# mLSTM heads in chunks of 256 tokens with three carried states, and two column sums folded into one set of matrix products

## The chip, the cores and the metric

One core of one Trainium2 chip. TensorE (PE) multiplies matrices, VectorE (DVE), ScalarE (ACT) and GpSimd (POOL) do elementwise work, and SyncE (SP) issues the DMAs. The built program sets the order of the instructions on each engine, and semaphores tell an instruction when what it needs is there. The metric is device microseconds of the whole program, a median over runs.

## The reference

One decoder layer over 1024 tokens of width 1024, in float32: an RMS norm, a projection into four mLSTM heads of width 128 and eight forgetting-attention heads of width 64, an output projection, cross-attention into 256 memory tokens, an MLP with squared ReLU, and a final norm. The change concerns the mLSTM heads. Each has a causal convolution with SiLU on q and k, input and forget gates, and a recurrence that the reference runs in chunks of 64 tokens:

```
scores = einsum('bhtd,bhsd->bhts', qc, kc) * exp(dmat - m_t[..., None])
num = einsum('bhts,bhsd->bhtd', scores, vc) + inter * einsum('bhed,bhtd->bhte', C, qc)
den = scores.sum(-1) + inter * einsum('bhd,bhtd->bht', n, qc)
h = num / maximum(abs(den), exp(-m_t))
C_new = decay * C + einsum('bhs,bhse,bhsd->bhed', wa, vc, kc)
n_new = decay * n + einsum('bhs,bhsd->bhd', wa, kc)
```

C is a 128 x 128 state, n a vector, m a running maximum. A kernel may choose another chunk length: inside a chunk the scores are computed directly, across chunks the state carries. The head's output is then normalised by its mean square and gated.

## The kernel before, in words

Every product with full precision is done as three products of rounded halves (`mm3`, lines 192 to 194): each operand is split into a high part, rounded by ACT (line 138), and a low remainder, subtracted by DVE (line 139).

The mLSTM part runs over four heads. For one head, `ml_project` (lines 666 to 687) does: `conv_silu` of k (projection in 48 products of 512 columns, two evictions by DVE at line 522, four taps at lines 525 and 527, tanh on ACT at line 529, line 530, and the split at lines 141 and 142), `fx_project(0)`, the state of the first 512 tokens in `carried` (four transposes at line 545, eight products at line 551), `conv_silu` of q, `fx_project(1)`, the state's effect on the second 512 tokens in `carry`, and the output gate's projection. `ml_head` then computes scores and values in two halves of 512 tokens; within a half the four key blocks reach 512, 384, 256 and 256 query columns. The sums over the 128 partitions of the squares and of the denominators are products with a column of ones (`sum_cols`, line 232), four for each of the two in each half.

The closing of a head (from line 628 on) is a generator which the next head's `ml_project` advances between its steps: the 8 x 128 factors are transposed on PE (line 257), copied (line 258), stored to `facd`, read back as a broadcast to all partitions for the first half (line 261) and then for the second (line 637), and DVE scales the head's output with them (lines 640 and 641). The broadcasts share one buffer, `r_a`.

The order of all this on each engine is not written by hand here. A scheduler in the tile framework places instructions by program order and by its own estimate of when each can start, and assigns buffers from pools: PSUM has one bank tagged mm, one m2, two tp, three sc and one ov, and `mm()` hands out mm, tp, m2, tp in turn. A tile that takes a bank waits for the last reader of the tile before it there. Small SBUF buffers have tags too (`r_c`, `r_b`, `r_f` two each, `r_a` one).

Of the kernel before, what the change touches and what calls it, by code (L numbers as in the profile page):

```python
# [44 lines left out]
def hybrid_layer(ctx: ExitStack, tc: tile.TileContext, a: dict, out: bass.AP):  # L45
# [50 lines left out]
    def ov_():  # L96
        return ps_tile("ov")
# [22 lines left out]
    ones = const("ones", [P, 1])  # L120
    g.memset(ones, 1.0)
# [167 lines left out]
    def mem_prepare():  # L289
# [16 lines left out]
        rsqrt_sums(acc, rcol_m, 2, 2)  # L306
# [152 lines left out]
    left = dram.tile([MLH, TH], F32, name="left")  # L459
# [4 lines left out]
    def gate_rows():  # L464
# [21 lines left out]
        w = run[0:MLH, 0:TH]  # L486
        s.activation(w, rel[0:MLH, 0:TH], AF.Exp, bias=neg[0:MLH, TH - 1 : TH])
# [46 lines left out]
    def carried(hd, y):  # L534

        cols = col("m", 8, 1)
        m0, m1, n_ = (cols[:, i : i + 1] for i in range(3))
        load(m0, rows[hd : hd + 1, TH - 1 : TH].broadcast_to([P, 1]))

        kw = w2("b")  # L540
        load(kw, left[hd : hd + 1].broadcast_to([P, TH]))
        v.scalar_tensor_tensor(out=kw, in0=y[:, :TH], scalar=0.5 * float(P) ** -0.5, in1=kw, op0=ALU.mult, op1=ALU.mult, accum_out=n_)
        kt = mm() if hd else ov_()
        for j in range(4):
            nc.tensor.transpose(kt[:, j * P : (j + 1) * P], kw[:, j * P : (j + 1) * P], ident)
        kh, kl = w2("d", dt=F32R), w2("e", dt=F32R)
        split(kh, kl, kt)
        ps = mm()
        for j in range(4):
            for t in (kl, kh):  # L550
                nc.tensor.matmul(ps[:, 0:256], t[:, j * P : (j + 1) * P], mv_of(hd, j), start=j == 0 and t is kl, stop=j == 3 and t is kh)
        c32 = w2("c", P)
        s.activation(c32, ps[:, P : 2 * P], AF.Copy)
        v.tensor_tensor(out=c32, in0=ps[:, 0:P], in1=c32, op=ALU.add)
        c2 = w2("p", 2 * P, F32R)
        hi, lo = c2[:, 0:P], c2[:, P:]

        v.tensor_scalar(out=n_, in0=n_, scalar1=0.5, scalar2=None, op0=ALU.mult)
        v.tensor_scalar(out=m1, in0=m0, scalar1=-1.0, scalar2=None, op0=ALU.mult)
        split(hi, lo, c32)  # L560
        return m1, (hi, lo), n_

    def carry(hd, q, y, m1, c, n_):

        e = w2("c")
        load(e, rows[hd : hd + 1, TH:].broadcast_to([P, TH]))
        s.activation(e, e, AF.Exp, bias=m1)
        ps = mm()
        mm3(ps, c, both(q, lambda t: t[:, TH:]), True, True)
# [1187 lines left out]
```

## Time and profile before

| | |
|---|---|
| median of 3 runs | 1512.55 us (1512.06 to 1512.98) |
| profiled execution, span | 1510.9 us |
| TensorE busy | 1498.5 us, 99% |
| VectorE busy | 1097.5 us, 73% |
| ScalarE busy | 717.5 us, 47% |
| GpSimd busy | 450.6 us, 30% |

The profiled execution's own time is its span, 1510.9 us from the first to the last instruction; the median of the runs is 1.65 us above it. The four heads lie between about 60 and 370 us. In the rows of the timeline the columns are start, duration, engine, line, operation, output <- inputs, shape, count, and in brackets the idle time ahead with what ended it. In the rows by stretch each engine's busy time stands with its number of instructions, then the granted TensorE clock, the DMA share and GB/s.

### The profile page before, as it was taken

The numbers are of one execution on the slowest core, as the hardware profiler recorded it, in microseconds if no ns is written. First come the engines' busy times: TensorE is split into PE (matmuls) and PEld (weight loads), VectorE is DVE, ScalarE is ACT, GpSimd is POOL, SyncE is SP. The second block draws the span as 40 slices with busy tenths as digits, with TensorE's granted clock in tenths as the row PEclk, the third lists the DMA queues.
The fourth block names the chain that finished last, engine by engine and source line by source line (L and its number), as shares of the span: only waits on it lengthen the run. The fifth ranks groups of instructions, "written<-read, shape, count | busy, mean of one in ns | idle before, by whom it ended". The sixth has DMA issues, their size and how long they took to land.

```text
span 1510.9 us, 21868 instructions
## 1 busy us (share of the span) xinstructions
PE 1498.5 (99%) x7708; PEld 1259.5 (83%) x7708; DVE 1097.5 (73%) x1743; ACT 717.5 (47%) x1347; POOL 450.6 (30%) x529
## 2 busy tenths in 40 slices
PE   9999999999999999999999999999999999999997
PEld 8988888889999888888888888888888888888887
DVE  7676676665799875844457988888887788777765
ACT  7343343334788773534444556565656332222134
POOL 0003030413466551001110033344433644343312
PEclk9999999999999999999999999999999999999999
DMA  5332333436889768533334446867766865555623
GB/s 209 117 114 91 115 100 127 129 130 169 279 253 270 218 199 291 198 123 119 119 119 133 154 136 237 281 244 265 272 243 235 352 258 221 223 223 223 251 84 112
DMA packets 114258, 288.33 MB, mean 191 GB/s; under 512 B 12882, under 2 KB 23436, under 8 KB 108516
## 3 DMA queue, kind: packets, MB, share of 16 engines
q1 hardware_dynamic: 113860, 286.83, 56.0%
q8 instruction: 60, 0.98, 0.3%
q14 instruction: 50, 0.41, 0.1%
q10 hardware_dynamic: 288, 0.11, 0.0%
HBM read 194.36 MB, written 92.53 MB: 190 GB/s over the span
## 4 chain that ended last, share of the span: by engine, by line
PE 98%; issue 0%; DVE 0%; DMA 0%; POOL 0%; ACT 0%; POOLq 0%; ACTq 0%; DVEq 0%
PE tp L194 9%; PE tp L193 9%; PE tp L192 9%; PE sc L192 7%; PE sc L194 7%; PE sc L193 7%; PE m L192 6%; PE m L194 6%; PE m L193 6%; PE mm L192 6%; PE mm L193 6%; PE mm L194 6%; PE ov L813 2%; PE ov L192 2%; PE ov L193 2%; PE ov L194 2%
## 5 line engine op out<-in xcount | busy, mean ns | idle before, releaser
L194 PE MATMUL tp<-act,wh 128*128 128x512 f32 (+1 forms) x456 | 178.5, 392 | 0.0
L192 PE MATMUL tp<-act,wl 128*128 128x512 f32 (+1 forms) x456 | 178.5, 392 | 0.0
L193 PE MATMUL tp<-act,wh 128*128 128x512 f32 (+1 forms) x456 | 178.5, 391 | 0.0
L138 ACT ACTIVATE wh<-wr 128x1024 fp32r<-128x1024 f32 (+3 forms) x96 | 92.7, 966 | 95.9 <-PE tp L194 36.6
L139 DVE TENSOR_TENSOR wl<-wr,wh 128x1024 fp32r<-128x1024 f32 (+3 forms) x96 | 113.9, 1187 | 14.5 <-ACT wh L138 14.4
L193 PE MATMUL mm<-act,wh 128*128 128x512 f32 (+1 forms) x320 | 122.6, 383 | 0.0
L192 PE MATMUL mm<-act,wl 128*128 128x512 f32 (+1 forms) x320 | 122.6, 383 | 0.0
L194 PE MATMUL mm<-act,wh 128*128 128x512 f32 (+1 forms) x320 | 122.3, 382 | 0.0
L192 PE MATMUL m<-act,wl 128*128 128x512 f32 (+1 forms) x312 | 119.5, 383 | 0.0
L193 PE MATMUL m<-act,wh 128*128 128x512 f32 (+1 forms) x312 | 118.9, 381 | 0.0
L194 PE MATMUL m<-act,wh 128*128 128x512 f32 (+1 forms) x312 | 118.8, 381 | 0.0
L192 PE MATMUL sc<-act,wl 128*128 128x512 f32 (+1 forms) x268 | 103.8, 387 | 0.0
L193 PE MATMUL sc<-act,wh 128*128 128x512 f32 (+1 forms) x268 | 103.7, 387 | 0.0
L194 PE MATMUL sc<-act,wh 128*128 128x512 f32 (+1 forms) x268 | 103.6, 387 | 0.0
L194 PEld LDWEIGHTS tp<-act,wh 128*128 128x128 f32 x456 | 85.7, 188 | 19.5
L193 PEld LDWEIGHTS tp<-act,wh 128*128 128x128 f32 x456 | 85.8, 188 | 19.0
L192 PEld LDWEIGHTS tp<-act,wl 128*128 128x128 f32 x456 | 85.7, 188 | 19.0
L1491 POOL TENSOR_TENSOR z<-wr 128x256 f32<-128x256 f32 x56 | 50.4, 921 | 147.6 <-DMA wr<-w_ff2q 140.8
L138 ACT ACTIVATE w<-wr 128x768 fp32r<-128x768 f32 (+2 forms) x31 | 25.5, 825 | 133.7 <-PE tp L194 69.2
L138 ACT ACTIVATE wh<-z 128x1024 fp32r<-128x1024 f32 (+2 forms) x55 | 52.5, 956 | 65.0 <-POOL z L1491 28.8
L139 DVE TENSOR_TENSOR wl<-z,wh 128x1024 fp32r<-128x1024 f32 (+2 forms) x55 | 65.9, 1198 | 10.1 <-ACT wh L138 10.1
L194 PEld LDWEIGHTS mm<-act,wh 128*128 128x128 f32 x320 | 60.2, 188 | 12.5
(673 smaller groups left out, 4207.9 us busy)
## 6 DMA issues: line engine op xcount, KB each, us to landing
act<-right SPq DMA_DIRECT2D x35, 1024.0 KB
right<-r_d SPq DMA_DIRECT2D x70, 256.0 KB
right<-w SPq DMA_DIRECT2D x56, 256.0 KB
wr<-w_ff2q SPq DMA_DIRECT2D x28, 512.0 KB
act<-fqk SPq DMA_DIRECT2D x48, 256.0 KB
wr<-w_in SPq DMA_DIRECT2D x20, 512.0 KB
wr<-w_ff SPq DMA_DIRECT2D x20, 512.0 KB
fqk<-r_p SPq DMA_DIRECT2D x32, 256.0 KB
```

Of the source, the lines that this page charges most:

```text
L138: s.activation(hi, src, AF.Copy)
L139: return v.tensor_tensor(out=lo, in0=src, in1=hi.bitcast(F32), op=ALU.subtract)
L192: nc.tensor.matmul(ps, w[1], x[0], start=first, stop=False, skip_group_check=more)
L193: nc.tensor.matmul(ps, w[0], x[1], start=False, stop=False, skip_group_check=more)
L194: nc.tensor.matmul(ps, w[0], x[0], start=False, stop=last, skip_group_check=more)
L813: nc.tensor.matmul(self.ov[:, c0:], self.fv[:, self.j], t[:, c0:], start=self.j == 0 and t is self.p[1], stop=self.last and t is self.p[0])
L1491: g.tensor_tensor(out=o, in0=x, in1=y, op=op)
```

## The change

Chunks become 256 tokens long, so three states are carried instead of one (after 256, 512 and 768 tokens). `carried` weighs k against three chunk ends, in place in k's own buffer, takes six transposes and twelve products, and combines the three states on DVE with decay factors that ACT exponentiates. `carry` applies them to three chunks of q. In `ml_head` each half consists of two chunks with two key blocks of 256 columns each. The squares and the denominators are each folded from 128 to 64 partitions by DVE, side by side into one tile, and summed by four products with a two-column pattern of ones. The memory's norm folds its sums too. `carry` now stands ahead of `fx_project(1)`.

```diff
+    units_ = const("ones", [P, 3])
+    ones, pair_ones = units_[:, 0:1], units_[:, 1:3]
...
-        rsqrt_sums(acc, rcol_m, 2, 2)
+        v.tensor_tensor(out=acc[:, :NM], in0=acc[:, :NM], in1=acc[:, NM:], op=ALU.add)
+        rsqrt_sums(acc, rcol_m, 2)
...
+    QC = 256
+    left = dram.tile([MLH, 3 * QC], F32, name="left")
...
     def carried(hd, y):
...
-        kt = mm() if hd else ov_()
-        for j in range(4):
-            nc.tensor.transpose(kt[:, j * P : (j + 1) * P], kw[:, j * P : (j + 1) * P], ident)
...
+        cols, more = col("m", 8, 1), col("mx", 8)
+        m0, m1, n_, d = cols[:, 0:3], cols[:, 3:6], more[:, 0:3], more[:, 3:5]
+        load(m0, rows[hd : hd + 1, QC - 1 : 3 * QC : QC].broadcast_to([P, 3]))
+        v.tensor_scalar(out=m1, in0=m0, scalar1=-1.0, scalar2=None, op0=ALU.mult)
+
+        for c in range(2):
+            s.activation(d[:, c : c + 1], m0[:, c + 1 : c + 2], AF.Exp, bias=m1[:, c : c + 1])
...
+        for c in range(3):
+            at = slice(c * QC, c * QC + QC)
+            v.scalar_tensor_tensor(out=y[:, at], in0=y[:, at], scalar=0.5 * float(P) ** -0.5, in1=lw[c // 2][:, c % 2 * QC : c % 2 * QC + QC], op0=ALU.mult, op1=ALU.mult, accum_out=n_[:, c : c + 1])
+        c32 = w2("c", 3 * P).rearrange("p (c d) -> p c d", c=3)
+        for at, n in ((0, 2), (2, 1)):
+            kt = mm() if hd or at else ov_()
+            kt = kt[:, : n * QC]
+            for j in range(2 * n):
+                i = at * QC + j * P
+                nc.tensor.transpose(kt[:, j * P : (j + 1) * P], y[:, i : i + P], ident)
+            kh, kl = w2("d", n * QC, F32R), w2("e", n * QC, F32R)
+            split(kh, kl, kt)
+            ps = mm()[:, : n * QC].rearrange("p (c e d) -> p c e d", c=n, e=2)
...
     def carry(hd, q, y, m1, c, n_):
...
+        for i in range(3):
+            hf, x = divmod(i + 1, 2)
+            x = slice(x * QC, x * QC + QC)
+            z = slice(0, QC) if i == 0 else x
+            s.activation(e[hf][:, z], e[hf][:, z], AF.Exp, bias=m1[:, i : i + 1])
+            mm3(ps[hf][:, z], both(c, lambda t: t[:, i]), both(q, lambda t: t[:, (i + 1) * QC : (i + 2) * QC]), True, True)
...
     def ml_head(hd, q, k, og, nums, accs_):
...
+                for j, z in ends:
+                    mm3(sp[:, z], both(k, lambda t: t[:, j * P : (j + 1) * P]), both(q, lambda t: t[:, hf * TH + c * QC :][:, :QC]), True, True)
...
-            ps = sc()
-            sum_cols(ps[:, 0:4], acc, 4)
-            sum_cols(ps[:, 4:8], sq, 4)
...
+            folded = w2("c")
+            for t, x in ((folded[0:64], sq), (folded[64:128], acc)):
+                v.tensor_tensor(out=t, in0=x[0:64], in1=x[64:128], op=ALU.add)
+            for t in range(4):
+                nc.tensor.matmul(ps[:, t], folded[:, t * P : (t + 1) * P], pair_ones, start=True, stop=True)
...
+        sums = carry(hd, q, yq, *state)
         fx_project(1, hd)
-        sums = carry(hd, q, yq, *state)
```

Lines of the changed kernel move: `mm3` is at 195 to 197, the split at 141 and 142 (144 and 145 with a scale), the conv's eviction at 528, its taps at 531 and 533, tanh at 535 and line 536, the weighing of k at 554, transposes at 561, state products at 569, the carry's loads at 585, the folded sums at 644, the closing's transpose at 260, its copy at 261, its DMAs at 262, 264 and 663, its scaling at 666 and 667.

The order moves in three places. First TensorE at the state of head 1. Before (m_219 is the first half of conv q, mm_1588 the transposed k, tp_1597 the state):

```order
L192 MATMUL m_219_1629<-act_102,wl_1624 128x512
L545 MATMUL mm_1588<-ident,r_b_1585 128x128
L193 MATMUL ov_1335<-r_e_1393,act_106 128x256
L194 MATMUL ov_1335<-r_d_1392,act_106 128x256
L545 MATMUL mm_1588<-ident,r_b_1585 128x128 x3
L193 MATMUL m_219_1629<-act_103,wh_1623 128x512
...
L194 MATMUL m_219_1629<-act_102,wh_1623 128x512
L551 MATMUL tp_1597<-act_106,r_e_1594 128x256
L551 MATMUL tp_1597<-act_106,r_d_1593 128x256
```

In the change (m_197 is the end of fx_project(0), tp_1612 and tp_1632 the transposed k, mm_1621 the states, tp_1670 conv q):

```order
L644 MATMUL sc_1419<-ones,r_c_1420 128x2 x4
L196 MATMUL m_197_1557<-act_107,wh_1521 128x512
L197 MATMUL m_197_1557<-act_106,wh_1521 128x512
L561 MATMUL tp_1612<-ident,z_188_1504 128x128 x4
L561 MATMUL tp_1632<-ident,z_188_1504 128x128 x2
L569 MATMUL mm_1621<-act_108,r_e_1618 128x256
L569 MATMUL mm_1621<-act_108,r_d_1617 128x256
...
L195 MATMUL tp_1670<-act_104,wl_1665 128x512
```

Between the transposes and the first product of the state 17 products of conv q stood before; now none does.

Second, TensorE from conv q to the carry of the same head in the change (mm_1696 is the second half of conv q, mm_1796 the second half of fx_project(1), tp_1739 and m_232_1740 the carry, tp_1764 the first half of fx_project(1); 24 products each for the halves):

```order
L197 MATMUL mm_1696<-act_106,wh_1664 128x512
L195 MATMUL mm_1796<-act_106,wl_1761 128x512
L196 MATMUL mm_1796<-act_107,wh_1760 128x512
...
L197 MATMUL mm_1796<-act_106,wh_1760 128x512
L195 MATMUL tp_1739<-act_1443,r_p_1652 128x256
L195 MATMUL m_232_1740<-act_1443,r_p_1652 128x256
L195 MATMUL tp_1764<-act_104,wl_1761 128x512
```

Before, both halves of fx_project(1) and 22 products of the output gate stood between conv q and the carry; now 24 products do, and they take the bank that conv q has just written.

Third, DVE at the same place. Before:

```order
L522 TENSOR_TENSOR z_218_1627<-tp_1655,row 128x512
L525 TENSOR_SCALAR z_221_1681<-z_218_1627,vec 128x1024
L139 TENSOR_TENSOR wl_2018<-wr_2015,wh_2017 128x1024
L527 SCALAR_TENSOR_TENSOR z_221_1681<-z_218_1627,vec,z_221_1681 128x1024 x2
L653 SCALAR_TENSOR_TENSOR r_p_1721<-mm_1696,row 128x512
L527 SCALAR_TENSOR_TENSOR z_221_1681<-z_218_1627,vec,z_221_1681 128x1024
L640 SCALAR_TENSOR_TENSOR r_f_1319<-r_f_1319,vec,r_a_1498 128x512
L641 SCALAR_TENSOR_TENSOR r_f_1319<-w_131_1188,r_f_1319 128x512
L530 SCALAR_TENSOR_TENSOR z_221_1681<-z_218_1627,z_221_1681 128x1024
```

In the change:

```order
L528 TENSOR_TENSOR z_221_1668<-tp_1670,row 128x512
L666 SCALAR_TENSOR_TENSOR r_f_1140<-r_f_1140,vec,r_a_1513 128x512
L667 SCALAR_TENSOR_TENSOR r_f_1140<-w_142_1233,r_f_1140 128x512
L545 TENSOR_SCALAR c_m_2196<-c_m_2196 128x3
L145 SCALAR_TENSOR_TENSOR r_f_1140<-r_f_1140,r_y_1591 128x512
L666 SCALAR_TENSOR_TENSOR r_f_1141<-r_f_1141,vec,r_a_1596 128x512
L528 TENSOR_TENSOR z_221_1668<-mm_1696,row 128x512
L667 SCALAR_TENSOR_TENSOR r_f_1141<-w_142_1233,r_f_1141 128x512
L142 TENSOR_TENSOR wl_2045<-wr_2042,wh_2044 128x1024
L531 TENSOR_SCALAR z_224_1722<-z_221_1668,vec 128x1024
L145 SCALAR_TENSOR_TENSOR r_f_1141<-r_f_1141,r_y_1657 128x512
L533 SCALAR_TENSOR_TENSOR z_224_1722<-z_221_1668,vec,z_224_1722 128x1024 x3
```

Both scalings of the previous head's closing (L666, with the broadcasts r_a) now stand ahead of the eviction of conv q's second half; before, they stood behind it.

120 lines of the change are left out of this document (58 added, 62 removed).

## The prediction

> **What bounds the kernel now.** I read the page first, then the busy time by stretches.
>
> ```profile
> span 1510.9 us, 21868 instructions
> PE 1498.5 (99%) x7708; PEld 1259.5 (83%) x7708; DVE 1097.5 (73%) x1743; ACT 717.5 (47%) x1347; POOL 450.6 (30%) x529
> ...
> PE 98%; issue 0%; DVE 0%; DMA 0%; POOL 0%; ACT 0%; POOLq 0%; ACTq 0%; DVEq 0%
> ...
> 171.00:241.00 70.00, 70.00 (x340) 58.33 (x339) 47.57 (x75) 25.65 (x43) 14.16 (x18) 1.00 0.34 108
> ```
>
> TensorE is never free, the chain of waits lies on it for 98%, and in the stretch of one mLSTM head (171 to 241 us, the last row) it works 70 of 70 us at full clock while VectorE (DVE) works 47.6. So the time is the sum of the slots that instructions take on TensorE, start to start, plus any wait that a new order puts on it. The timeline gives the slots:
>
> ```profile
> 200.00 0.39 PE L193 MATMUL m<-act,wh 128*128 128x512 f32 x1
> 200.24 0.39 PE L194 MATMUL m<-act,wh 128*128 128x512 f32 x1
> ...
> 201.41 0.34 PE L192 MATMUL sc<-act 128*128 128x384 f32 x1
> 201.59 0.34 PE L193 MATMUL sc<-act 128*128 128x384 f32 x1
> ...
> 203.65 0.28 PE L193 MATMUL ov<-r_e,act 128*128 128x256 f32 x1
> 203.77 0.28 PE L194 MATMUL ov<-r_d,act 128*128 128x256 f32 x1
> ...
> 209.85 0.95 PE L232 MATMUL sc<-ones,r_c 128*128 128x1 f32 x8
> 210.66 0.37 PE L192 MATMUL sc<-act 128*128 128x256 f32 x1
> ...
> 222.41 0.60 PE L545 MATMUL tp<-ident,r_b 128*128 128x128 f32 x4
> 222.76 0.48 PE L192 MATMUL tp<-act,wl 128*128 128x512 f32 x1
> ```
>
> 512 columns take 0.235 us, 384 take 0.177, 256 take 0.12, a column sum 0.10 (eight in 0.81), a transpose 0.09 (four in 0.35). The 0.28 to 0.39 of the rows is latency, and overlaps.
>
> **What TensorE saves.** Scores and values, per half: three products each of 512, 384, 256 and 256 columns, twice: 6 x (0.235 + 0.177 + 0.12 + 0.12) = 3.9 us; now 24 of 256, 2.9. Eight halves: -8.2. Column sums fall from 64 to 32: -3.2. The memory norm's, from 4 to 2: -0.2. The states cost 4 more products of 256 columns and 2 more transposes per head, 4 x (0.48 + 0.18) = +2.6, and the carry 9 x 0.12 against 3 x 0.235, 4 x 0.375 = +1.5. Sum -7.5 us. The folds, the extra exponentials and the chunked splits are on DVE, ACT and POOL, which have 22 us and more of slack in the 70; they cost nothing so long as TensorE does not stand behind them. That is what the new order changes.
>
> **What the order adds: the head's closing.** In the change the product of the second half of conv q writes bank mm, and so does the next block, the 24 products of fx1. There is one such bank, so they wait for the eviction L528, and on DVE L528 now stands behind the second L666, which waits for a broadcast of the head's factors. How long that takes shows in head 0's closing now:
>
> ```profile
> 170.43 0.27 PE L257 MATMUL sc<-ident,c_fac 128*8 128x128 f32 x1
> ...
> 170.73 0.27 ACT L258 ACTIVATE r_a<-sc 8x128 f32<-8x128 f32 x1 [2.77 <-PE sc L257]
> ...
> 171.03 0.28 SPq L259 DMA_DIRECT2D facd<-r_a  x1
> 173.34 0.32 SPq L261 DMA_DIRECT2D r_a<-facd  x1
> 177.35 0.32 SPq L637 DMA_DIRECT2D r_a<-facd  x1
> ...
> 176.57 0.75 DVE L640 SCALAR_TENSOR_TENSOR r_f<-r_f,vec,r_a 128x512 f32<-128x512 f32 x1 [2.08 <-DMA r_a<-facd]
> 180.64 0.75 DVE L640 SCALAR_TENSOR_TENSOR r_f<-r_f,vec,r_a 128x512 f32<-128x512 f32 x1 [0.85 <-DMA r_a<-facd]
> ```
>
> Store 2.3 us, load 3.2, and, since there is one buffer r_a, a second load of 3.3 after the first is used: the second scaling begins 10.2 us after the transpose of the factors and ends at 10.95. L528 (0.69, below) ends at 11.65. After the same transpose TensorE has 5 + 24 products, 0.25 + 29 x 0.235 = 7.05 us. **Wait C: 4.6 us.** If the three DMAs went a quarter faster, 2.4 us would be left of it; if the small load of c_m, which on SP stands ahead of the second factor load and itself follows an exponential, came late by its own 2.7 us (row below), 7.3. The carry's own second load now stands on SP between the store and the load of the factors; it waits for the state's split, 0.4 us after the transpose, and the factor load waits 2.3 us for the store anyway, so it holds nothing up.
>
> **The carry.** It now stands directly behind those 24 products and begins with q's rounded half. What is between the eviction of conv q and that half, in the trace of now:
>
> ```profile
> 166.90 0.69 DVE L522 TENSOR_TENSOR z<-tp,row 128x512 f32<-128x512 f32 x1 [1.41 <-PE tp L194]
> 167.62 0.81 DVE L525 TENSOR_SCALAR z<-z,vec 128x1024 f32<-128x1024 f32 x1
> 168.35 1.22 DVE L139 TENSOR_TENSOR wl<-wr,wh 128x1024 fp32r<-128x1024 f32 x1
> 169.49 2.60 DVE L527 SCALAR_TENSOR_TENSOR z<-z,vec,z 128x1024 f32<-128x1024 f32 x2
> ...
> 177.97 1.22 DVE L530 SCALAR_TENSOR_TENSOR z<-z,z 128x1024 f32<-128x1024 f32 x1
> ...
> 174.58 1.06 ACT L529 ACTIVATE z<-z 128x1024 f32<-128x1024 f32 x1 [3.58 <-DVE z L527]
> 179.22 1.06 ACT L141 ACTIVATE act<-z 128x1024 fp32r<-128x1024 f32 x1 [0.51 <-DVE z L530]
> ...
> 183.13 0.39 PE L192 MATMUL m<-act,r_p 128*128 128x512 f32 x1
> ```
>
> Now q is ready at 180.28, 13.4 us after the eviction began, and its carry is issued at 183.13: 70 products stand between, so nobody waits. In the new order the DVE rows after L528 (shown above) are L667 0.69, a weights split 1.22, L531 0.81, the closing's L145 0.68, three L533 3.9, then tanh 1.06, L536 1.22, ACT's rounding 1.06: 10.6 us, less about 0.08 where one row starts before the one ahead ends: 10.4. TensorE has 24 x 0.235 = 5.6. **Wait D: 4.8 us**; 3.0 without the weights split and L145, 5.5 with some delay at each hand-over. The rest of the carry needs q's remainder, two DVE pieces later, with 20 products ahead of it: covered.
>
> **The states.** The transposes L561 come directly after fx0's last products, and the state products L569 directly after the transposes, since conv q needs the two tp banks that the transposes hold. Nearest rows for the pieces:
>
> ```profile
> 88.39 0.60 ACT L138 ACTIVATE r_d<-ov 128x512 fp32r<-128x512 f32 x1 [1.49 <-PE ov L545]
> ...
> 89.35 0.67 DVE L139 TENSOR_TENSOR r_e<-ov,r_d 128x512 fp32r<-128x512 f32 x1
> 111.02 0.15 DVE L559 TENSOR_SCALAR c_m<-c_m 128x1 f32<-128x1 f32 x1 [1.28 <-DMA c_m<-rows]
> ...
> 108.28 0.39 SPq L538 DMA_DIRECT2D c_m<-rows  x1
> ...
> L823 DVE TENSOR_TENSOR r_f<-r_c x16: 686/745/1229, 402.8 to 573.4; 64x512 f32<-64x512 f32 x16
> ```
>
> From the eviction of conv k's second half to the second L554, DVE now has: eviction 0.69, L531 0.81, weights 1.22, taps 3.9, the sum L636 0.69, two folds of 64x512 at 0.75, two fx0 evictions 1.4, L536 1.22, two splits 1.9, small ones 0.3, two half-wide L554 some 0.8 (an estimate from 0.69 for the full width), and 0.8 of waiting for ACT: 15.2, with the overlaps 14.9 to 15.9. TensorE has 48 x 0.235 + 12 x 0.12 + 0.4 = 13.1. **Wait A: 2.2 us** (0 to 3.5). Then the split that L569 needs stands behind the third L554, a reciprocal, a weights split, another split and two small ones: 0.4 + 0.16 + 1.22 + 0.69 + 0.35 + 0.67 = 3.5, less overlap 0.3, against six transposes of 0.55. **Wait B: 2.6 us**; at the least the two rows above, 1.27 less two transposes, 1.1.
>
> Head 0 has no closing behind it and other work beside the states. Its L528 costs latency 0.17 plus 0.69, and its carry the chain without L667 and L145, 9.4 against 5.85, that is 3.6, and up to 3 more because L545 (the next head's c_m) stands in it: exponentials, a load of 3.2 and the c_m load of 2.7 (108.28 to 111.02) come first. I take 1 + 5 = 6.
>
> **The clock.** A wait can cost more than its length:
>
> ```profile
> 1499.75 0.28 PE L194 MATMUL sc<-act,w 128*128 128x256 f32 x1
> ...
> 1.24 4.46 PE L118 MATMUL ov<-r_y 128*128 128x512 bf16 x11 [1.24 <-DVE r_y L115]
> ...
> 1502.00:1504.00 2.00, 0.47 (x2) 0.50 (x3) 0.49 (x4) 0.00 (x0) 0.71 (x1) 0.90 0.38 131
> 1504.00:1510.00 6.00, 0.64 (x3) 0.34 (x2) 2.55 (x5) 0.00 (x0) 0.00 (x0) 0.50 0.51 175
> ```
>
> About 3.6 us after the last dense product (mean 0.90 over 1502 to 1504) the granted clock halves; at the start eleven products of 512 columns take 4.46 us, 0.17 each over the 0.235, so coming back costs 11 x 0.17 = 1.9 us. A and B together leave 5.4 us without a dense product, head 0's carry 5: four losses of 1.9, 7.6 us. One after C is hidden, since D waits for DVE anyway. The Trainium skill (TensorE: Matmul & The Clock Gate, Part 1: The HAM clock gate) puts it at half clock after an idle window of about 3.4 us, and the trace's 3.6 agrees; by that page alone D would lose it too.
>
> **Sum.** (2.2 + 2.6 + 4.6 + 4.8) x 3 = 42.6; head 0, 6; clock 7.6; TensorE's saving 7.5: +48.7 us on 1510.9, that is 1559.6. The median of the runs is 1.65 above the profiled span: **1561 us**, slower by 3.2%.
>
> **Rivals.** (1) *The waits are covered.* For it: DVE is busy 47.6 us of 70, and in the stretch quoted TensorE never waits. Against: C is three DMAs in a row behind a single buffer, and the order leaves 29 products after the transpose. Then -7.5: 1505. Chance 0.07, and 0.02 for a tie at little change. (2) *Only the bare latencies remain*: A 0, B 1.1, C 2.4, D 3.0, head 0 3.6 + 0.9, no clock loss: 3 x 6.5 + 4.5 - 7.5 = +16.5, 1529. Chance 0.15. (3) *The clock falls after D as well*: 5.7 more, 1567; the end of the trace speaks for it, but D's wait shrinks if the clock is still low in the 24 products before. 0.16. (4) *SP's queue*: the c_m load ahead of the second factor load is late, C becomes 7.3: +8, 1569. Against it: its exponentials should end before L666. 0.08.
>
> **Chances and range.** The forecast has 0.52, from 1545 to 1566. The range 1533 to 1575 takes in (3), (4) and the upper part of (2). Differences under 0.2%, 3 us, are no change for this measurement: faster 0.07, same 0.02, slower 0.91.
>
> **What would show it.** In the waits of the changed kernel, TensorE must wait for DVE before L561 and L569 (2 to 3 us each, three heads), for DVE at the first fx1 product (4 to 5) and for ACT at the carry (4 to 5, four heads); TensorE's busy time must fall; the granted clock in the stretch from 90 to 380 us must drop below 1.00. If the stretch stays at 100% busy, the sum of waits is wrong as a whole; if TensorE waits but for DMA in other places, (4). If all waits are there at half size, my DVE pieces overlap more than the rows show.

## The result and the profile after

The changed kernel takes 1565.4 us (median of 4 runs, 1562.5 to 1566.6) against 1512.3 us (4 runs, 1511.9 to 1513.0): a ratio of 1.0344, 95% interval 1.0332 to 1.0357. The forecast was 1561 us, slower, with a range from 1533 to 1575. The profiled execution has 1560.8 us against 1510.9, 49.9 us more. One execution of experiment 1 below, the profiled one, took 2126.2 us at a granted clock of 0.65 and is left out of its numbers, which is why the same kernel stands there a second time as experiment 9.

From the page of the changed kernel: its span, the busy times, and the clock that TensorE was granted, in tenths over 40 slices.

```profile
span 1560.8 us, 21877 instructions
...
PE 1510.5 (97%) x7688; PEld 1263.8 (81%) x7688; DVE 1114.0 (71%) x1784; ACT 715.7 (46%) x1357; POOL 445.7 (29%) x531
...
PEclk9989898999999999999999999999999999999999
```

TensorE has 20 instructions fewer, and yet its busy time rose from 1498.5 to 1510.5 us: that is the clock in the main, since products take longer at half of it. The prediction had named a falling busy time as a sign of being right; this sign did not come. By stretches (columns: length, then PE, PEld, DVE, ACT, POOL busy, granted clock, DMA share, GB/s):

```profile
110.00:180.00 70.00, 60.90 (x285) 50.28 (x286) 42.33 (x72) 22.16 (x38) 11.86 (x18) 0.88 0.23 77
180.00:265.00 85.00, 75.12 (x344) 61.26 (x343) 51.87 (x85) 25.70 (x45) 11.87 (x18) 0.92 0.30 95
265.00:350.00 85.00, 76.17 (x347) 61.53 (x345) 52.56 (x86) 26.51 (x47) 15.49 (x21) 0.92 0.36 110
350.00:420.00 70.00, 64.19 (x422) 58.12 (x422) 41.65 (x70) 25.40 (x51) 18.93 (x24) 0.95 0.43 126
420.00:480.00 60.00, 58.90 (x456) 55.87 (x455) 45.96 (x113) 41.66 (x115) 25.55 (x43) 1.00 0.89 279
```

The loss lies in the four mLSTM heads, where TensorE had worked almost without a gap: it is now idle 8 to 13% of the time, at a clock of 0.88 to 0.95; behind 420 us its waits are those of before. What it waits for (waits over the whole program: total us, times, longest):

```profile
PE mm L195 <- DVE z L528: 12.1, 4, 4.2
PE tp L195 <- ACT w L144: 8.9, 2, 7.1
PE mm L569 <- DVE r_e L142: 6.2, 3, 2.2
PE tp L195 <- ACT act L144: 5.0, 2, 3.1
PE tp L561 <- DVE z L554: 3.4, 3, 1.1
PE ov L561 <- DVE z L554: 2.3, 1, 2.3
```

These are the places forecast: C (12.1, with 0.7 of head 0), D (8.9 and 5.0, with 7.1 of head 0), B (6.2), A (3.4), and one that was not forecast, head 0's own transposes (2.3). Head 1 in the timeline, TensorE, VectorE and SyncE's queue, and ScalarE:

```profile
185.35 0.39 PE L197 MATMUL mm<-act,wh 128*128 128x512 f32 x1
189.51 0.80 PE L195 MATMUL mm<-act,wl 128*128 128x512 f32 x1 [3.77 <-DVE z L528]
...
196.36 0.40 PE L197 MATMUL mm<-act,wh 128*128 128x512 f32 x1
199.90 0.58 PE L195 MATMUL tp<-act,r_p 128*128 128x256 f32 x1 [3.15 <-ACT act L144]
...
183.86 0.75 DVE L666 SCALAR_TENSOR_TENSOR r_f<-r_f,vec,r_a 128x512 f32<-128x512 f32 x1 [2.98 <-DMA r_a<-facd]
...
186.80 0.17 DVE L545 TENSOR_SCALAR c_m<-c_m 128x3 f32<-128x3 f32 x1 [1.46 <-DMA c_m<-rows]
186.87 0.69 DVE L145 SCALAR_TENSOR_TENSOR r_f<-r_f,r_y 128x512 fp32r<-128x512 f32 x1
188.10 0.75 DVE L666 SCALAR_TENSOR_TENSOR r_f<-r_f,vec,r_a 128x512 f32<-128x512 f32 x1 [0.55 <-DMA r_a<-facd]
188.77 0.68 DVE L528 TENSOR_TENSOR z<-mm,row 128x512 f32<-128x512 f32 x1
...
184.64 0.40 SPq L663 DMA_DIRECT2D r_a<-facd  x1
...
198.79 1.06 ACT L144 ACTIVATE act<-z 128x1024 fp32r<-128x1024 f32 x1 [1.29 <-DVE z L536]
```

TensorE ends conv q at 185.6 and stands until L528 has evicted it, and L528 stands behind the second scaling, which waits for the second factor load (184.64 to 188.10). That is C. From the end of L528 (189.45) to q's rounded half (199.85) VectorE and ScalarE take 10.4 us; TensorE has 24 products for it. That is D.

To compare whole programs I split every gap between two starts on TensorE into three: the slot that this form takes at full clock (its median), the excess of products that began at half clock, and, where more than 0.15 us is left, a wait. The sums of each profiled execution, us (what the three leave of the span, 7.7 to 8.0 us, lies before the first product and behind the last). The split is good to about 1 us. One product, the two-column transpose ahead of head 0's C (L260), occurs too seldom for a median, so that the wait behind it counts as its slot: 0.8 us in the change, 3.9 us in experiment 4.

| kernel | median | ratio to before, 95% interval | span | slots | waits | clock |
|---|---|---|---|---|---|---|
| before | 1512.3 | | 1510.9 | 1496.9 | 5.9 | 0.2 |
| the change | 1565.4 | 1.0344 (1.0332 to 1.0357) | 1560.8 | 1488.7 | 46.6 | 17.7 |
| 1, 9: carry back | 1552.6 to 1556.1 | 1.0270 (1.0252 to 1.0287) | 1554.5 | 1486.9 | 44.0 | 15.7 |
| 2: move alone | 1520.9 | 1.0051 (1.0036 to 1.0066) | 1520.5 | 1496.9 | 14.0 | 1.7 |
| 3: two factor buffers | 1560.6 | 1.0312 (1.0297 to 1.0327) | 1556.7 | 1489.5 | 43.7 | 15.6 |
| 4: c_m's own tile | 1569.5 | 1.0361 (1.0333 to 1.0389) | 1568.0 | 1491.9 | 50.0 | 18.4 |
| 5: folds alone | 1517.1 | 1.0024 (1.0011 to 1.0037) | 1516.6 | 1490.5 | 12.8 | 5.4 |
| 6: transposes early | 1541.7 | 1.0188 (1.0174 to 1.0202) | 1541.5 | 1486.9 | 37.4 | 9.3 |
| 7: spread order | 1513.2 | 1.0001 (0.9992 to 1.0010) | 1511.2 | 1485.6 | 16.6 | 1.2 |
| 8: filled waits | 1567.1 | 1.0360 (1.0346 to 1.0374) | 1566.7 | 1493.9 | 46.4 | 18.5 |
| 10: 7, scalings as before | 1516.7 | 1.0016 (1.0007 to 1.0025) | 1515.1 | 1486.2 | 16.2 | 4.7 |
| 11: 7, gate's own buffer | 1516.1 | 1.0023 (1.0013 to 1.0032) | 1514.7 | 1486.7 | 17.2 | 3.0 |
| 12: 11 without folds | 1511.9 | 0.9992 (0.9983 to 1.0001) | 1513.5 | 1494.2 | 10.1 | 1.5 |

So the change saves 8.2 us of slots, adds 40.7 us of waits and 17.5 us of clock: 50.0 of the 49.9. (The ratios of the experiments are taken against runs of the kernel before on the same chip, 1512.5 to 1513.3 us.)

### The profile page after: what moved, and what is told of

It is laid out like the page before. It is cut to its first block, busy times and chain, and to the rows that moved or that the text cites. A ratio compares the mean times of both kernels' runs of the same rounds, so it can differ in the third digit from the quotient of the medians.

```text
span 1560.8 us, 21877 instructions
## 1 busy us (share of the span) xinstructions
PE 1510.5 (97%) x7688; PEld 1263.8 (81%) x7688; DVE 1114.0 (71%) x1784; ACT 715.7 (46%) x1357; POOL 445.7 (29%) x531
## 4 chain that ended last, share of the span: by engine, by line
PE 75%; DVE 1%; DMA 1%; issue 0%; ACT 0%; POOL 0%; POOLq 0%; DVEq 0%; ACTq 0%; SPq 0%
PE tp L195 6%; PE sc L195 6%; PE sc L196 6%; PE sc L197 6%; PE tp L196 6%; PE tp L197 6%; PE m L195 5%; PE m L196 5%; PE m L197 5%; PE mm L195 4%; PE mm L197 4%; PE mm L196 4%; PE ov L839 2%; PE tp L819 2%; PE ov L195 2%; PE ov L197 2%
## 5 line engine op out<-in xcount | busy, mean ns | idle before, releaser
L195 PE MATMUL tp<-act,wl 128*128 128x512 f32 (+1 forms) x456 | 182.3, 400 | 0.0
L196 PE MATMUL tp<-act,wh 128*128 128x512 f32 (+1 forms) x456 | 181.6, 398 | 0.0
L197 PE MATMUL tp<-act,wh 128*128 128x512 f32 (+1 forms) x456 | 180.7, 397 | 0.0
L195 PE MATMUL mm<-act,wl 128*128 128x512 f32 (+1 forms) x336 | 132.6, 395 | 12.2 <-DVE z L528 12.1
L196 PE MATMUL mm<-act,wh 128*128 128x512 f32 (+1 forms) x336 | 131.3, 391 | 0.0
L197 PE MATMUL mm<-act,wh 128*128 128x512 f32 (+1 forms) x336 | 130.9, 390 | 0.0
L195 PE MATMUL m<-act,wl 128*128 128x512 f32 (+1 forms) x296 | 113.0, 382 | 0.0
L196 PE MATMUL m<-act,wh 128*128 128x512 f32 (+1 forms) x296 | 112.7, 381 | 0.0
L197 PE MATMUL m<-act,wh 128*128 128x512 f32 (+1 forms) x296 | 112.4, 380 | 0.0
L196 PEld LDWEIGHTS tp<-act,wh 128*128 128x128 f32 x456 | 88.1, 193 | 19.9 <-issue 0.2
L197 PEld LDWEIGHTS tp<-act,wh 128*128 128x128 f32 x456 | 87.7, 192 | 20.2
L1517 POOL TENSOR_TENSOR z<-wr 128x256 f32<-128x256 f32 x56 | 55.2, 1007 | 147.1 <-DMA wr<-w_ff2q 131.1
L195 PEld LDWEIGHTS mm<-act,wl 128*128 128x128 f32 x336 | 64.9, 193 | 26.9 <-DVE z L528 13.8
L197 PEld LDWEIGHTS mm<-act,wh 128*128 128x128 f32 x336 | 64.8, 193 | 14.0
```

Of the source, the lines that this page charges most:

```text
L195: nc.tensor.matmul(ps, w[1], x[0], start=first, stop=False, skip_group_check=more)
L196: nc.tensor.matmul(ps, w[0], x[1], start=False, stop=False, skip_group_check=more)
L197: nc.tensor.matmul(ps, w[0], x[0], start=False, stop=last, skip_group_check=more)
L1517: g.tensor_tensor(out=o, in0=x, in1=y, op=op)
```

## The experiments

**1 and 9: the carry back behind fx1.**

```diff
-        sums = carry(hd, q, yq, *state)
         fx_project(1, hd)
+        sums = carry(hd, q, yq, *state)
```

> The change with its last line undone: the carry stands behind fx1 again, all else as in the change. Theory 1 (the prediction's C and D: TensorE runs out of products while VectorE still prepares q): 48 products of fx1 now stand between conv q and the carry, 11.3 us. From the transpose of the factors to q's rounded half the changed kernel's trace has 178.71 to 199.90, 21.2 us; TensorE has 5 + 24 + 48 products there, 18.1 us. So C is gone, D stays at 3 us in three heads, head 0's 7.2 us falls to about 2, and with A and B as they are the time is 1565.4 - 11.9 (C) + 1 x 3 (D: from about 2.4 to about 3) - 0.6 - 5 (head 0) - some 6 of clock = about 1543 (1535 to 1550). Rival (the move is all of the loss): A and B too are only what the new order leaves uncovered, and the time falls to 1505 to 1520. Second rival (three states need more of VectorE, wherever the carry stands): C and D come back at the scores, and the time stays above 1558.

Measured: 1.0270, some 11 us less than the change, between theory 1 (1543) and its second rival. The same kernel once more, for its trace:

> The kernel of the first experiment once more, for its trace. It fell by 11 us and not by the 22 that theory 1 gave. Theory 3 (a new wait took D's place): with 48 products of fx1 ahead of it the carry no longer waits for VectorE, but ScalarE rounds the next block's weights ahead of q, and that weight buffer is free only when fx1's last product is done, so TensorE stands for two roundings of 1.06 us and the hand-overs, 2.1 to 2.6 us, in each head; A and B stand as in the change (1.3 and 2.2). Theory 1 with a longer chain (VectorE is later than 18.1 us): ScalarE is not busy with weights there, and its rounding of q begins as soon as VectorE's L536 ends.

Its waits of TensorE (total us, times, longest):

```profile
PE tp L195 <- ACT w L144: 7.8, 2, 4.6
PE tp L195 <- ACT act L144: 6.5, 2, 3.3
...
PE tp L196 <- DVE act L145: 2.5, 2, 1.3
PE tp L196 <- DVE w L145: 1.7, 1, 1.7
```

And its timeline in head 1, TensorE and ScalarE:

```profile
193.06 0.40 PE L197 MATMUL m<-act,wh 128*128 128x512 f32 x1
196.81 0.58 PE L195 MATMUL tp<-act,r_p 128*128 128x256 f32 x1 [3.35 <-ACT act L144]
...
193.35 1.06 ACT L535 ACTIVATE z<-z 128x1024 f32<-128x1024 f32 x1 [5.57 <-DVE z L533]
194.31 1.04 ACT L141 ACTIVATE wh<-wr 128x1024 fp32r<-128x1024 f32 x1
195.70 1.06 ACT L144 ACTIVATE act<-z 128x1024 fp32r<-128x1024 f32 x1 [0.35 <-DVE z L536]
```

Theory 3 falls: ScalarE's weights (194.31) follow the tanh without a wait, and q's rounding waits for VectorE. Theory 1 stands: C is gone, and D is 3.2 to 3.4 us in heads 1 to 3 (3 forecast). But it left three things out. q's remainder (L145), which in the change has 20 products ahead of it, is now wanted two products after the rounded half: 1.3 to 1.7 us in each of these heads. Head 0's carry still waits 4.6 us (7.1 in the change, 2 forecast). And 2.9 us of waits are new behind the heads (1.8 us at 498 us, 1.1 at 1005). In the profiled executions waits fell by 2.6 us only, clock by 2.0, slots by 1.8, 6.3 us together where the medians differ by 11. Putting the carry back is not the remedy.

**2: the move alone**, on the kernel before (the diff of 1 the other way round).

> The kernel before with nothing but the carry's call moved ahead of fx1. Theory 1 (the move costs because in the change only 24 products are left between conv q and the carry): in this kernel the written-out order still leaves 68 products (one block of 24 of fx1, 24 of og, 20 of fx1) between them, more than the 44 that 10.4 us need, so the time stays within 5 us of 1512.5 and no wait of over 1 us appears at the carry. Rival (the move alone costs what the change costs): C and D of some 4 + 3 us in three heads, head 0's 7, and clock losses: 1540 or more.

Measured: 1.0051, 8 us slower, between the two. No wait stands at a carry, as theory 1 had it; the 8.1 us of new waits lie at other places. The longest, 2.1 and 1.8 us at 334 and 338 us, are of C's kind: VectorE's eviction L653 at 332.95 stands behind a scaling of the previous head's closing (L640 at 332.15), which had waited 3.1 us for its factors. So the move is not free even where its own wait is covered: alone it costs 8 us, a seventh of the loss, and undone in the change (experiment 1) it gives 11, a fifth.

**3: a second buffer for the factors.**

```diff
-        fbs = [w2("a"), w2("d")] if end else [None, None]
+        fbs = [w2("a"), w2("d" if end else "y")]
...
             if hf == 0:
                 to_row(fb, fac, 8, at, sc)
-            if hf != end:
-                load(fbs[1] or fb, at[:, TH:].broadcast_to([P, TH]))
+                load(fbs[1], at[:, TH:].broadcast_to([P, TH]))
...
-            yh, yl = w2("e" if end and hf else "y", dt=F32R), y.bitcast(F32R)
+            yh, yl = w2(("ye" if end else "ay")[hf], dt=F32R), y.bitcast(F32R)
```

> The change, with the second half's factors in a buffer of their own, so that both broadcasts are loaded right after the store; the rounded first half takes over the other buffer. TensorE's and VectorE's order in head 1 to 3 stay as they are. Theory as predicted (C is three DMAs in a row behind a single buffer): the second load's 3.3 us leave the chain, C falls from 3.9 to about 0.6 us in three heads, D stays, so 10 us less, 1555, and with clock regained after C down to 1551. Rival (C is held by something else as well: in the changed kernel's trace VectorE waits at 186.80 for the next head's c_m, 1.3 us before the second factors are there): C falls by 0.6 to 1.3 us only, and the time by 2 to 4 us: 1561 to 1564.

Measured: 1560.6 us, 5 less. VectorE in head 1:

```profile
182.16 0.75 DVE L665 SCALAR_TENSOR_TENSOR r_f<-r_f,vec,r_a 128x512 f32<-128x512 f32 x1 [2.90 <-ACT r_c L592]
182.82 0.74 DVE L665 SCALAR_TENSOR_TENSOR r_f<-r_f,vec,r_y 128x512 f32<-128x512 f32 x1
184.85 0.17 DVE L545 TENSOR_SCALAR c_m<-c_m 128x3 f32<-128x3 f32 x1
185.53 0.68 DVE L528 TENSOR_TENSOR z<-mm,row 128x512 f32<-128x512 f32 x1
```

Both scalings now follow each other, the second factors wait for nothing, and C falls from 3.9, 3.7 and 4.3 us to 2.3, 2.6 and 3.1: by 1.3, not by 3.3. The rival's number came, but not by its reason. c_m's negation (L545) waits for 0.2 us at most in this run, and head 3, which has none, keeps the longest C. What holds L528 now is VectorE's own work: from the first scaling, which starts late because its factors come late (idle 2.9 us ahead of it; the row names ScalarE, but the factor load issued at 178.91 lands then, and heads 2 and 3 name the load), to L528 VectorE works almost without a pause, 3.4 us in head 1 (182.16 to 185.53) and 3.4 to 3.5 in the others. The wait for the second factors through the single buffer was 1.1 to 1.6 us of C; the rest is these rows and the place that the order gives to L528 behind them.

**4: c_m in a tile of its own.**

```diff
-        m0, m1, n_, d = cols[:, 0:3], cols[:, 3:6], more[:, 0:3], more[:, 3:5]
+        m0, m1, n_, d = more[:, 5:8], cols[:, 3:6], more[:, 0:3], more[:, 3:5]
```

> The change, with the loaded c_m in another small tile, so that the next head's load of it does not wait for this head's exponentials. VectorE's order changes with it: c_m's negation comes ahead of the first scaling, and the eviction of conv q's second half ahead of the second scaling instead of behind it. TensorE's order stays. Theory (one chain: the second factor load, at 188.10 in the changed kernel, stands ahead of the rest of q's work, wherever the eviction stands): C falls from 3.9 to about 0.7 us, but D grows by about the same, from 2.0 to 3.3 now to 5 or more, and the time falls by 0 to 4 us: 1561 to 1566. Rival (each wait has its own cause, and D is only q's own chain): C falls to 0.7, D stays, and the time falls by 9 to 12 us, 1553 to 1556.

Measured: 1569.5 us, not faster (1562.8 to 1570.9). In head 1 the eviction indeed moved ahead of the second scaling (which still starts at 187.03); the other two rows are head 0's:

```profile
184.48 0.68 DVE L528 TENSOR_TENSOR z<-mm,row 128x512 f32<-128x512 f32 x1
...
187.03 0.75 DVE L666 SCALAR_TENSOR_TENSOR r_f<-r_f,vec,r_a 128x512 f32<-128x512 f32 x1 [1.09 <-DMA r_a<-facd]
...
103.91 0.17 DVE L545 TENSOR_SCALAR c_m<-c_mx 128x3 f32<-128x3 f32 x1 [4.12 <-ACT r_c L592]
...
104.73 0.50 PE L195 MATMUL mm<-act,wl 128*128 128x512 f32 x1 [3.79 <-DVE z L528]
```

In head 1 C fell from 3.9 to 1.8 us and D grew from 3.3 to 7.5: one chain, as the theory said, and the wait moved with a loss. In heads 2 and 3 the eviction stays behind the second scaling, and C did not fall (3.8 and 5.3; 3.7 and 4.3 in the change). In head 0 the carry's wait fell from 7.2 to 2.2 us, but C grew from 0.7 to 3.8: only the load has moved. The negation L545 still writes the tile that the exponentials L592 read, waits for them, and now stands ahead of L528 instead of behind it. So head 0 gained 1.9 us and not 5, and a wait of 2.5 us at 513 us and longer D's in all other heads took more than that; why D grew in heads 2 and 3 stays open. The slots of the table, 3 us above the change's, are no real slots: they hold head 0's C (see above the table).

**5: the folds alone**, on the kernel before: the fold of squares and denominators with its 4 products per half, and the memory norm's addition, word for word as in the change.

> The kernel before with only the folds of the change: squares and denominators folded to 64 partitions each and summed in one product per 128 tokens, and the memory norm's two halves added before its sums. Blocks, state and order of calls as before. Theory (the saving of TensorE's slots is real where nothing is moved): 34 column sums fewer at 0.10 us, -3.4 us, 1509.1 (1508 to 1510.5). Rival (the sums now wait for two folds of 0.75 us on VectorE, and TensorE's order around them has no cover): no gain or slower, 1512 to 1516.

Measured: 1517.1 us, slower by 0.24% (its six executions lie between 1513.2 and 1520.2). The slots fell by 6.4 us, twice what was forecast: a sum or a fold's product is two instructions on TensorE (64 records of L624 for the 32 products of the eight halves), so that 68 were saved at 0.10 us and not 34. But

```profile
PE tp L555 <- DVE r_e L142: 2.8, 2, 1.4
PE sc L624 <- DVE r_c L622: 2.0, 1, 2.0
```

6.9 us of new waits and 5.2 us of clock came with them. The second row is the sum that waits for its fold. The first is the state, and here the folds are not the cause: its split on VectorE (157.38 to 158.06) stands ahead of both folds (158.09 and 158.88, 0.69 us each). The split stands behind the eviction of the last value product (L613), and this order leaves no product of conv q between that product and the state. So most of the 6.9 us stand where the order changed with the folds; what the folds themselves cost shows in experiment 12.

**6: the transposes called before conv q, the state products after it.** `carried` becomes a generator that stops behind the splits:

```diff
             split(kh, kl, kt)
+            parts.append((at, n, kh, kl))
+        yield
+        for at, n, kh, kl in parts:
...
         state = carried(hd, yk)
+        next(state)
         next(closing, None)
         yq = conv_silu(hd, *q)
+        state = next(state)
         sums = carry(hd, q, yq, *state)
```

> The change, with the state's transposes and splits still called before conv q, but the products of the state after it. In the order that results, 20 products of conv q stand ahead of the transposes and 28 between them and the state products; the carry stays ahead of fx1. Theory (A and B are VectorE being late for products without cover, and lengthen the program by their own length and by the clock they cost): A falls from 1.3 and B from 2.2 us to 0 in three heads, head 0's 2.5 goes too, 13 us and some 5 us of clock less, 1547 (1543 to 1552), with C and D together as long as now. Rival (VectorE is the bound from fx0 to the carry, so that what A and B no longer wait is waited for at C and D): C and D grow by the same 3.5 us per head, and the time stays above 1558.

Measured: 1541.7 us, 24 less than the change, a little more than the theory's range gave. No wait is left at the transposes or between them and the state products; of the span's 19.3 us, waits give 9.2, clock 8.4, slots 1.8. C and D together are 7.9, 6.5 and 8.6 us (7.2, 5.6 and 6.4 in the change): they took back some 4 us, not the 10 of the rival. The wait ahead of fx1 has another cause now:

```profile
PE mm L195 <- DVE r_c L576: 14.8, 4, 6.0
```

L576 combines the states, which lie in bank mm behind conv q in this order. So the theory's mechanism holds: A, B and head 0's 2.5, some 12 us of waits, were worth 19 us in the profiled executions, after what C and D took back, and 8 of that was clock.

**7: all of the work in another order.** Beside 4 and 6:

```diff
-            kt = mm() if hd or at else ov_()
-            kt = kt[:, : n * QC]
+            kt = sc()[:, : n * QC]
...
         fx_project(0, hd)
-        next(closing, None)
...
         yq = conv_silu(hd, *q)
-        sums = carry(hd, q, yq, *state)
+        close_behind()
+        close_behind()
         fx_project(1, hd)
+        state = next(state)
         og = w4()
...
+        sums = carry(hd, q, yq, *state)
```

`close_behind` takes one step of the closing and orders its first instruction on VectorE behind the last one issued, q's remainder.

> Everything of the change's arithmetic (three states, 256-token blocks, folds), in another order: the transposes write banks of the scores and are called before conv q, the state products after fx1, the carry after the output gate's products; both factor scalings are held behind q on VectorE; c_m's load has its own tile. Theory (the chunking saves TensorE 8.2 us, and all of the loss is order): no wait of over 1 us in the four heads beside those of the kernel before, clock at 1.00 there, 1505 (1503 to 1510), below the kernel before. Rival (VectorE and ScalarE have too much to do for 256-token blocks in any order, since they work 71% and 48% of the time on average but all of the stretch between conv q and the scores): waits of 2 us or more per head remain, 1513 or more.

Measured: 1513.2 us, no difference from the kernel before (0.9992 to 1.0010), and 52 us less than the change. So order made nearly all of the loss, but the forecast of 1505 was missed: the 11.3 us of slots that are now saved went to waits of 10.7 us. The time is the rival's (1513 or more), but its waits of 2 us or more in every head are not there; beside head 2's none in the heads is above 0.7 us. The two largest:

```profile
PE m L195 <- DVE w L727: 4.1, 1, 4.1
PE sc L799 <- ACT act L812: 3.4, 3, 1.4
```

The first is head 2's: a product of the next head waits for the output gate's eviction, which stands on VectorE behind the two scalings, since the gate's buffer is the previous head's. The second lies behind the heads (377 to 505 us), where TensorE waits for ScalarE in the attention; why it is longer than in the kernel before (0.7 us) was not followed up.

**8: unread products in head 3's waits.** `fill` issues n products of 512 columns into a bank that nobody reads, ordered behind what was issued last:

```diff
+            last = fill(idle, 15, products()[-1].name)
             sums = carry(hd, q, yq, *state)
             fx_project(1, hd)
+            held(block[len(block) // 2], last)
+            held(first, fill(idle, 7, block[-1].name))
```

> The change with products that nobody reads put into two of the waits of head 3: 15 of 512 columns (3.5 us) between conv q and fx1 (C), 7 (1.6 us) between fx1 and the carry (D). They leave the results alone; TensorE's order before them is the same. Theory as predicted (the clock lost after C is hidden, since D waits for VectorE in any case): the granted clock no longer drops in head 3 behind C, the 24 products of fx1 take 5.6 us instead of about 8.3, and the carry begins as late as now after conv q's last product (14.7 us from 349.36 to 364.1), so the time is the same within 1.5 us: 1564 to 1567. Rival (every half-clock stretch lengthens the program): the carry begins 2.7 us earlier, 1562 to 1563.

Measured: 1567.1 us. In head 3:

```profile
359.62 0.39 PE L197 MATMUL mm<-act,wh 128*128 128x512 f32 x1
...
364.55 0.58 PE L195 MATMUL tp<-act,r_p 128*128 128x256 f32 x1 [2.92 <-ACT act L144]
```

The products of fx1 run at 0.235 us again, and the carry begins at 364.55; everything ahead lies 0.7 us later than in the change, where it begins at 364.3, so it is 0.5 us earlier, not 2.7. The theory holds in this head: the clock lost behind C is hidden in D. But the granted clock now drops behind D instead (from 363.8 for 6.8 us; in the change it was full from 359.8 on), where no longer wait follows. Here a wait that was shortened for TensorE alone only moved the slow stretch to a worse place.

**10 to 12: variants of 7.** In 10 the scalings of the even heads are not held behind q, and the factors have two buffers as in 3; in 11 head 2's gate has another buffer; 12 is 11 with the sums unfolded again.

```diff
+        close_behind(hd % 2)
...
-        og = w4()
+        og = quarters()[0] if hd == 2 else w4()
```

> The spread order of the seventh experiment, with two differences for head 2, where TensorE waited 4.3 us at 256 us for the eviction of the output gate (its buffer is the previous head's, free only after both scalings, which were held behind q): in the head whose q and k lie in the five wide buffers the scalings are not held back, and the second half's factors have a buffer of their own. Theory (that wait was all that stood between the spread order and its 1505): it falls below 1 us, and with it a clock loss of 1 us, 1508 (1505 to 1511). Rival (the evictions are late because VectorE has no time there, so the wait moves to the scores): 1512 to 1516.

Measured: 1516.7 us. L727's wait is gone, but in head 2 TensorE now waits 1.6 and 1.4 us for q (the scores, from L144 and L145), and 2.4 us in head 3 for a fold:

```profile
PE sc L661 <- DVE r_c L659: 2.4, 1, 2.4
PE sc L195 <- ACT w L144: 1.6, 1, 1.6
```

> The spread order of the seventh experiment, where the only large wait was head 2's: 4.1 us before a product whose bank held the output gate, its eviction on VectorE behind both factor scalings, since the gate's buffer was the previous head's. Here head 2's gate lies in another buffer (a quarter of the tile that held the gates' rows), the rest as in the seventh. Theory (order alone decides): the eviction moves ahead of the scalings, the 4.1 us and the clock lost with them (some 1.2 us) go, 1508 (1505 to 1510.5), below the kernel before. Rival (as in the tenth, VectorE is too full between conv q and the scores of this head, and another product waits instead): 1512 to 1516.

Measured: 1516.1 us. Head 2's 4.1 us are gone, and in head 3 two others stand in their place, again a fold and the eviction of a carry:

```profile
PE sc L661 <- DVE r_c L659: 2.6, 2, 2.4
PE m L195 <- DVE r_f L614: 2.3, 1, 2.3
```

Both times the time came out where the rival had it, a little above 1516, and another product waits instead. That VectorE has too much work there is shown only in part: ahead of L614 in experiment 11 it stands idle for 2.0 us itself, at a split of the closing that waits for ScalarE, which in turn waits 3.5 us for the store out of its buffer r_y.

> The kernel of the eleventh experiment without the folds of squares and denominators (they are summed by 64 column products again, as before the change; the memory norm's halves are still added). Theory 4 (in the stretch from conv q to the scores VectorE is the bound of the 256-token blocks, so its time there is worth more than TensorE's): the folds' 16 x 0.75 us of VectorE are worth more than the 32 column sums of 0.10 us that they save, the waits of 2.5, 2.6, 1.2 and 1.4 us in heads 2 and 3 shrink by more than the 3.2 us that TensorE has more: 1509 (1506 to 1512). Theory 1 in its simple form (TensorE's slots are what counts, the rest is luck of the order): 3 us slower than the eleventh, 1517 to 1521.

Measured: 1511.9 us, 4 less than 11, though TensorE has 7.5 us of slots more; in the profiled executions (this kernel's is the slowest of its eleven) waits fall by 7.1 us and clock by 1.5. In the four heads only one wait, of 0.75 us, is left of 6.3 us. Theory 4 holds for the folds: their VectorE time was worth more than the slots that they save. Against the kernel before it is 0.9992 (0.9983 to 1.0001): no difference that can be told. So the best version of the 256-token blocks with three states is as fast as the kernel before, and none was found that beats it.

## Why the prediction was right, and where its steps were not

**TensorE's saving**: 7.5 us forecast, 8.2 measured, which is luck in part. The prediction took a column sum for one instruction; it is two, so the folds save 6.4 us (experiment 5) and not 3.4, and experiment 7, with few waits, saves 11.3 in all. In the change some 3 us of this do not appear: 0.8 us is the wait that the split takes for a slot, the rest probably short delays of under 0.15 us at each restart, which it also counts as slots.

**Wait A**, 2.2 us in three heads, was 1.1 (3.4 in all), within its bounds. VectorE reaches the end of the second L554 about as summed (152.64 to 167.5, 14.9 us for 15.2), but the transposes wait only for the first (they start at 167.23), and TensorE's products ahead of them take 0.4 us more than the 13.1 that were summed. **Wait B**, 2.6, was 2.1. Both were there for the reason given, and experiment 6 shows it by taking them away.

**Wait C**, 4.6, was 3.8 (12.1 less 0.7, in three). The place, the bank and the eviction behind the second scaling were as forecast. The reason was a part of it: the second load through the one buffer is worth 1.3 us (experiment 3); the rest is the first scaling's late start and 3.4 us of VectorE's own rows, which the order puts ahead of L528. Rival 4 (C 7.3) did not happen: c_m is there 1.3 us before the second factors come.

**Wait D**, 4.8, was 3.1, 1.8 and 1.9. VectorE's chain is exactly as summed: 10.4 us in the rows above. What was wrong is the other side, 24 products in 5.6 us: after C the clock is at half, and they took 7.1, 8.5 and 8.4 us (from 189.51 to 196.6 in head 1). The prediction said that a clock loss after C is hidden since D waits anyway, and then did not take it off D.

**Head 0**, 6 us, was 10.1: 0.7 at L528, 7.1 at the carry, 2.3 at the transposes. The carry's bounds were 3.6 to 6.6; c_m's load holds VectorE for 3.5 us there (L545 at 107.12), more than the 3 that were allowed for. Experiment 4 takes 5 us off the carry by moving the load, and 3.1 of them come back at L528. That head 0's transposes would wait was not forecast at all ("other work beside the states"): its work is there, but stands behind them.

**The clock**, 7.6 us, was 17.5: nine drops instead of four. The step that failed is the condition, "about 3.6 us after the last dense product". Waits of 1.1 and 2.2 us with six transposes between them are enough, and so is head 0's 2.5 (below). Of the 17.5 us some 7 lie behind C and are no loss of their own, since they shorten D; that is rival 3's caution, and experiment 8 shows it for head 3. Rival 3 itself, the drop behind D, came in one head of three (head 1, at 199.4 us).

So the waits were 7.9 us too long (48.6 for 40.7), the clock 9.9 us too short, the slots 0.7 off: the sum, +48.7, came to within 1.3 us of the 50.0 in the main because two errors cancel: C's clock was left out of the clock term, and not taken off D. That closeness is luck; the median, 1565.4, lies 4.4 us above the forecast. The direction and the size rest on the right mechanism, TensorE out of products while VectorE is late; the split between waiting and clock was wrong. Rival 1 was wrong for this order, and right as a possibility only: in experiment 7 the waits are covered to three quarters. Rival 2 was too low, since nothing of the clock was in it and its waits, 24 us, were too short for the 40.7.

## What to carry to other kernels

An engine that was 73% busy on average can still be the bound in the one stretch where the new work falls: price added VectorE work (here 16 folds of 0.69 us and, in all, 41 instructions more) in that stretch, from the row where its input is ready to the row that TensorE needs, and count the products that the order leaves in between. Saved matmul slots are worth their time only if the order keeps covering; a wait that is removed at one bank comes back at the next consumer of the same chain unless the chain gets shorter. Where short waits come in clusters, add what the clock will cost: here 40.7 us of waits brought 17.5 us of it, and taking away A, B and head 0's 2.5 gave 9.2 us of waits and 8.4 of clock. Do not count the clock again where a longer wait follows at once.

## What the runs showed of the hardware

The granted clock moves on a grid. In the twelve traces of the change and of experiments 2 to 12 there are 60 drops to 0.50 inside the program; each lasts one, two or three times 3.41 us, and within a trace they begin at whole multiples of 3.41 us from each other. Windows cut on that grid in the changed kernel (length, TensorE busy, granted clock, DMA share, GB/s):

```profile
165.25:168.66 3.41, 1.99 (x11) 1.00 0.15 55
168.66:172.08 3.42, 1.55 (x7) 0.50 0.74 216
172.08:175.49 3.41, 3.41 (x11) 0.50 0.32 118
175.49:178.90 3.41, 3.41 (x19) 1.00 0.00 0
247.17:250.58 3.41, 2.29 (x15) 1.00 0.27 102
277.88:281.30 3.42, 2.54 (x11) 1.00 0.00 0
```

The first window holds A and part of B, and the next is slow; a full window brings the clock back. The fifth, too, is followed by a slow one, the sixth is not. Busy spans do not sort them, since they reach into the waits.

Slots do, if products of at most twelve columns are not counted; nearly all of these are the column sums, one or two columns wide. Take 0.235 us for a product of 512 columns, 0.177 for 384, 0.12 for 256, 0.11 for a transpose, twice that at half clock, and then the share that these fill of each window of the grid in the twelve traces. The 60 windows ahead of a drop lie at 0.395 or below, the 5169 other windows at full clock at 0.396 or above. At half clock, the 60 windows ahead of the return to full clock lie at 0.81 or above, the 35 others at 0.75 or below. The first, fifth and sixth window shown have 0.33, 0.35 and 0.69. With the sums counted the fifth has 0.58, and windows with and without a drop mix from 0.40 to 0.58. This is a fit to the traces and no experiment was made on it; whether a transpose counts they do not settle, since leaving it out sorts them as well.

So the idle time needs to be neither 3.4 us long nor in one piece: in 53 of the 60 windows no pause of TensorE reaches 3 us, and in the fifth shown the longest is 1.1. The Trainium skill (TensorE: Matmul & The Clock Gate, Part 1: The HAM clock gate) has a free-running window of 3413 ns, and the grid agrees; it speaks of an idle window, and here a window that was a third full was enough.
